# Value weights beside ones in an attention's second product, a guard term as a full-height product, and four-tap sums kept in PSUM

## The chip, the cores and the metric

The kernel runs on one core of one Trainium2 chip. The metric is the device time of one execution in microseconds (us), taken as the median of several runs. One execution was also recorded by the hardware profiler, and all rows below come from that recording. TensorE multiplies matrices, VectorE and ScalarE do elementwise work and can reach PSUM (the accumulators of TensorE), GpSimd does elementwise work in SBUF alone, and SyncE issues most of the transfers.

## What is computed

The reference is a two-layer backbone over 1024 latent tokens and 256 context tokens, all in float32, with a model width of 1024. Each layer has a token mixer of two parallel halves and then a gated feed-forward part. The change touches layer 1's mixer: its recurrence and its latent attention. It also touches how PSUM is handed out.

```python
def rglru_direction(u_lat, u_ctx, conv_w, conv_b, gate_w, gate_b, lam, reverse):
    pad = (0, LRU_CONV_WIDTH - 1) if reverse else (LRU_CONV_WIDTH - 1, 0)   # width 4
    def coeffs(u):
        xc = dwconv(u, conv_w, conv_b, pad[0], pad[1])                       # four taps
        r = jax.nn.sigmoid(block_diag(xc, gate_w[0], gate_b[0]))
        i = jax.nn.sigmoid(block_diag(xc, gate_w[1], gate_b[1]))
        ...
    h_lat = linear_scan(a_l, b_l, h0, reverse)

def one_block(args):                                   # 8 heads, 64 + 32 features
    s_lat = (einsum('bqhd,bshd->bhqs', qn, k_nope) + einsum('bqhr,bsr->bhqs', qr, k_rope)) * scale
    s_ctx = (einsum('bqhd,bshd->bhqs', qn, kc_nope) + einsum('bqhr,bsr->bhqs', qrr, kc_rope)) * scale
    p_lat, p_ctx = joint_softmax([s_lat, s_ctx])
    return einsum('bhqs,bshd->bqhd', p_lat, v) + einsum('bhqs,bshd->bqhd', p_ctx, vc)
```

## The kernel before

**Precision.** Most matrix products are made of three fp32r products of a high and a low part (lines 305 to 307, and the score products of the attention). P·V, the row sums and the recurrence's gates are plain float32, which the profile records as two records for one product.

**Order of the work.** The program text gives a priority order. A planner in the framework then orders the instructions of each engine by that priority and by estimated costs, and each engine runs its list strictly in that order. Generators (`spawn`, `pump`, `next(side)`) interleave background work with the matrix products.

**Recurrence (`lru`, `taps`, from line 975).** While the projections of layer 1's mixer run, it works on four groups of 128 channels. For a group, `taps` loads 1283 columns (1024 latent, 3 between, 256 context) into `xb` and makes, for each of two directions, one first product (line 997) and three multiply-and-add instructions (line 1001) on VectorE, all with their sum in SBUF. The next group's taps are made in the middle of a group. The gates are float32 products of 128x128 weights (line 1019), and GpSimd multiplies the input gate with the convolved input (line 1022). Layer 0's convolution (line 640) uses the same multiply-and-add instruction, with its sum in a three-bank PSUM tile `ca`.

**Attention (`mla`, `head`, from line 1352).** Eight heads, two groups of 512 queries, ten tiles of 128 keys (eight latent, two context): 160 steps. A step makes scores in `st` (three fp32r products of 128x512; a context tile has a fourth of one row, line 1376, that subtracts the query's guard). ScalarE takes the exponential into `p` (line 1378). P·V (line 1362) has the 64 value columns of the head as weights, and splits the 512 queries into halves: one half lands in partitions 0 to 63 of the bank `po`, the other in 64 to 127, so two matmuls use different column halves of TensorE's array. The row sums of P are built by elementwise addition, by the letters of `ACC`: six tiles on GpSimd (five additions), four on VectorE (three additions), and one closing addition (line 1395). Then two products with a matrix of ones (line 1398) put the row sums into `po`, VectorE takes the reciprocal (128x256, line 1400) and multiplies twice (64x256, line 1404). The guard of the next queries (`guard`, lines 1305 to 1331) runs in between: products into `sx` (lines 1312 and 1317, two banks), whose maxima VectorE takes (lines 1313 and 1319). `side` and `tail` interleave the next head's projections, its guard and the last head's end with the present head's scores.

**PSUM.** There are eight banks. `psum_pools` closes the pools before and opens new ones. In the attention they are sx, st, po and mm, two banks each; around it mm has four and `big` two of two banks each. Layer 0's projections use `ca` in the place of `big`.

Of the kernel before, what the change touches and what calls it, by code (L numbers as in the profile page):

```python
# [11 lines left out]
F32 = mybir.dt.float32  # L12
# [39 lines left out]
CY = 7.0  # L52
VS = (2, 2, 2, 2, 3, 3, 3, 3, 1, 1)
GK = 1
ACC = "GVGGVGGVGV"
PVD = 4
PB1 = 6
VW = 3
# [41 lines left out]
def tile_backbone(ctx: ExitStack, tc: tile.TileContext, a: dict, out: bass.AP):  # L100
# [25 lines left out]
        return f"{s}{uid[0]}"  # L126

    psum_pools(mm=4)
    cap = ExitStack()
    psum["ca"] = cap.enter_context(tc.tile_pool(name="cap", bufs=1, space=PSUM))  # L130
    ctx.callback(lambda: psx[0].close())

    def page(shape, dt=F32, s="pg"):
        return pgp.tile(shape, dt, tag="pg", name=nm(s))
# [463 lines left out]
    def mixer0(hs, nxt, xs0):  # L598
        w = a["ab_w_in"][0]
        pc = ph[0]  # L600
        rcos, rsin = pc.tile([128, 1024], F32, name="rcos", bufs=1), pc.tile([128, 1024], F32, name="rsin", bufs=1)
        protr = pc.tile([128, 3, 128], F32R, name="protr", bufs=1)
        with tc.tile_pool(name="m0a", bufs=1) as pa:
            prep = proj0(hs, w, pa, rcos, rsin, protr, xs0)
        cap.close()
        psum["big"] = psx[0].enter_context(tc.tile_pool(name="big0", bufs=2, space=PSUM))
        cat = Lazy()
        with tc.tile_pool(name="m0b", bufs=1) as pb:
            attn0(pb, *prep, cat)
        ws[0] = "o0"  # L610
        with tc.tile_pool(name="m0o", bufs=8 * len(YPO)) as po:
            for i, g in enumerate(GO0):
                if i < 2:
                    spawn(cat.load(GO0[i + 1]), "cat")
                ys, sq, last = outproj(a["ab_w_out"][0], cat, g, (lambda g: [po.tile([128, 512], F32, tag="y", name=nm("y")) for _ in range(8)]) if g in YPO else (lambda g: acts(g, 8, F32, "y")), lambda g: PO0[g], range(7, -1, -1) if g in OR0 else None)
                drain("cat")
                spawn(update(0, g, ys, sq, 2, last, True, (0, 3, 4) if g < 2 else None, nxt, PU0[g]))
            pumping[0] = True
            while not posted >= {(0, g) for g in YPO}:
                advance(flows["norm"])  # L620
            pumping[0] = False

    def proj0(hs, w, pa, rcos, rsin, protr, xs0):
        def conv(i, U):
            wc = lambda k: cols("acw", k * 4 + i)
            A = psum["ca"].tile([128, 1536], F32, tag="ca", name=nm("ca"))[:, 0:CW]
            B = None
            S.activation(A, U[:, 15:15 + CW], AF.Identity, scale=wc(15), bias=cols("acb", i))
            taps = [k for k in range(31) if k != 15]
            pt, dt = taps[:PTAPS], taps[PTAPS:]  # L630
            nch = 6
            for c in range(nch):
                for k in pt[c::nch]:
                    P = pa.tile([128, CW], F32, tag="cp", name=nm("cp"), bufs=2)
                    G.tensor_scalar(P, U[:, k:k + CW], wc(k), 1.0, ALU.mult, ALU.mult)
                    if B is not None:
                        G.tensor_add(P, P, B)
                    B = P
                for k in dt[c::nch]:
                    V.scalar_tensor_tensor(A, U[:, k:k + CW], wc(k), A, ALU.mult, ALU.add)  # L640
                yield CY
            O = pa.tile([128, CW], F32, tag="co", name=nm("co"), bufs=2)
            V.tensor_add(O, A, B)
            for g in range(3):
                nc.sync.dma_start(cd[g][:, i], O[:, COFF[g]:COFF[g] + TOK[g]])
# [334 lines left out]
    def lru(todo, x5, GW, sp, tiny, done):  # L980
# [4 lines left out]
        def taps(i):  # L985
# [7 lines left out]
            for d in range(2):  # L993
                x = x5("xc", 4)[:, 0:XW]
                XC.append(x)
                tap = lambda k: cols("lcw", (d * 4 + k) * 4 + i)
                V.tensor_scalar(x, XB[:, 3:3 + XW], tap(0 if d else 3), cols("lcb", d * 4 + i), ALU.mult, ALU.add)
                for k in range(4):
                    o = k + 3 if d else k
                    if o != 3:  # L1000
                        V.scalar_tensor_tensor(x, XB[:, o:o + XW], tap(k), x, ALU.mult, ALU.add)
            return XC

        XN = None
# [46 lines left out]
    def mixer1(hs, nxt):  # L1051
# [6 lines left out]
        G.memset(KR[64:128], 0.0)  # L1058
        G.memset(KR[96:97, 0:SEQ], -1.0)
        wv = []  # L1060
        with tc.tile_pool(name="m1a", bufs=1) as pa:
            proj1(hs, w, pa, tab, KR, wv)
        with tc.tile_pool(name="m1b", bufs=1) as pb:
# [131 lines left out]
    def mla(pc, tab, KR, wv):  # L1195
# [39 lines left out]
        scale = float(96 ** -0.5)  # L1235
        Q = {}

        VA = pc.tile([128, 10, 512], F32, name="va")

        def v_all(side):  # L1240
            wh, wl = wv
            for t in range(10):
# [4 lines left out]
                for k in range(2):  # L1247
# [2 lines left out]
                    T.matmul(ps, ch, rh, start=k == 0, stop=False)  # L1250
                    T.matmul(ps, ch, rl, start=False, stop=False)
                    T.matmul(ps, cl, rh, start=False, stop=k == 1)
                (S.copy if t % 2 else V.tensor_copy)(VA[:, t], ps)

        def split_s(raw, key, after=None):
            hi, lo = (pc.tile([128, raw.shape[1], 128], F32R, tag=key + x, name=nm(key), bufs=1) for x in "hl")
# [28 lines left out]
        def q_piece(h, g):  # L1285
# [11 lines left out]
            qh, ql, qc = (x[:, sl] for x in Q[h])  # L1297
            S.copy(qh, q)
            V.tensor_sub(qc, q, f32(qh))
            G.tensor_sub(ql[0:96], q[0:96], f32(qh[0:96]))  # L1300
            yield


# [48 lines left out]
        def head(h, g):  # L1352
            qh, ql, qc = (x[:, OFF[g]:OFF[g] + 512] for x in Q[h])
            kh, kl, kc = K[h % NK]
            po = psum["po"].tile([128, 512], F32, tag="po", name=nm("po"))
            accs, P = {}, []

            def pv(t):
                p = P[t]
                v = VA[:, t, h * 64:h * 64 + 64]  # L1360
                for b in range(2):
                    T.matmul(po[64 * b:64 * b + 64, 0:256], v, p[:, 256 * b:256 * b + 256], start=t == 0, stop=t == 9)  # L1362

            for t in range(10):
                st = psum["st"].tile([128, 512], F32, tag="st", name=nm("st"))
# [5 lines left out]
                else:  # L1371
# [1 line left out]
                    T.matmul(st, b_, qh, start=True, stop=False)  # L1373
                    T.matmul(st, a_, qh, start=False, stop=False)
                    T.matmul(st, a_, qc, start=False, stop=False)
                    T.matmul(st, kh[96:97, 0:128], ql[96:97], start=False, stop=True)
                p = pc.tile([128, 512], F32, tag="p", name=nm("p"), bufs=PB1)
                S.activation(p, st, AF.Exp, scale=scale)
                P.append(p)
                e = ACC[t]  # L1380
                if e not in accs:
                    accs[e] = p
                else:
                    n = pc.tile([128, 512], F32, tag="ac" + e, name=nm("ac"), bufs=2) if accs[e] in P else accs[e]
                    (G if e == "G" else V).tensor_add(n, accs[e], p)
                    accs[e] = n
                if t % 2 and t > PVD:
                    pv(t - PVD - 1)
                    pv(t - PVD)
# [1 line left out]
            for t in range(10 - PVD, 10, 2):  # L1391
                pv(t)
                pv(t + 1)
                yield
            V.tensor_add(accs["V"], accs["V"], accs["G"])
            yield
            for b in range(2):
                T.matmul(po[64 * b:64 * b + 64, 256:512], ones[:, 0:64], accs["V"][:, 256 * b:256 * b + 256], start=True, stop=True)
            rs = pc.tile([128, 256], F32, tag="rs", name=nm("rs"), bufs=2)
            V.reciprocal(rs, po[:, 256:512])  # L1400
            p0 = 64 * (h % 2)
            for b in range(2):
                o = OFF[g] + b * 256
                V.tensor_mul(att[h // 2][p0:p0 + 64, o:o + 256], po[64 * b:64 * b + 64, 0:256], rs[64 * b:64 * b + 64])
            if h % 2 and g:
                nc.sync.dma_start(attd[:, h // 2], att[h // 2])

        W, att, guarded, now = {}, {}, set(), [0]
        side = leads()
        psum_pools(sx=2, st=2, po=2, mm=2)  # L1410
        v_all(side)
        tail = iter(())
# [18 lines left out]
        for _ in tail:  # L1431
            pass
        drain("mul")
        psum_pools(big=2, mm=4)
        cat = Lazy()

        def load(g):
# [359 lines left out]
```

## Time and profile before

| | us |
|---|---|
| median of 3 runs | 3179.36 |
| lowest and highest | 3178.3, 3186.16 |
| profiled execution | 3171.12 |
| its span, first to last instruction | 3169.3 |

Busy time over the span: TensorE 2983.8 us (94%), VectorE 1879.2 (59%), GpSimd 1130.6 (36%), ScalarE 1115.0 (35%). The mean granted clock of TensorE was 0.966 of 2.4 GHz; it stands at either 1.2 or 2.4 GHz. A busy share counts a matmul from its start to its modelled end, and matmuls overlap, so the distance from start to start tells more of TensorE's stream than the busy time.

### The profile page before, as it was taken

How to read it: one execution, taken by the hardware profiler on the slowest of the kernel's cores; microseconds unless marked ns; L12 is line 12 of the kernel's file. 1: busy time of each engine (PE TensorE's matmuls, PEld its weight loads, DVE VectorE, ACT ScalarE, POOL GpSimd, SP SyncE). 2: the span in 40 equal slices, each digit the busy share in tenths (PEclk: the TensorE clock that was granted, in tenths of full speed). 3: DMA queues.
4: the chain of work that ended last, by engine and by line, in shares of the span. 5: the costliest groups of instructions: out<-in, count | busy, mean ns of one | idle time of the engine just before them, and what ended most of it. 6: DMA issues, size and time to landing. Idle time of an engine off the chain costs nothing. (4 is left out here: it accounts for less than half of the span.)

```text
span 3169.3 us, 38550 instructions
## 1 busy us (share of the span) xinstructions
PE 2983.8 (94%) x14825; PEld 2351.7 (74%) x14825; DVE 1879.2 (59%) x2842; ACT 1115.0 (35%) x1653; POOL 1130.6 (36%) x809
## 2 busy tenths in 40 slices
PE   6997999799999999988999779999998999999998
PEld 4886767678888888888987555555586888888886
DVE  5899986674654545577556977677636222223234
ACT  5214874532122111245533753233344322111213
POOL 4666546810111001165442344434444222122223
PEclk8998999899999999999999889999998999999999
DMA  7442004432333233346544230000053121111212
GB/s 283 130 135 91 28 15 143 144 109 73 94 100 93 75 90 102 113 147 202 159 132 130 89 98 26 31 31 27 33 167 100 53 60 47 33 48 54 60 40 106
DMA packets 321269, 292.50 MB, mean 92 GB/s; under 512 B 26065, under 2 KB 279678, under 8 KB 321086
## 3 DMA queue, kind: packets, MB, share of 16 engines
q1 hardware_dynamic: 317280, 287.14, 28.8%
q10 hardware_dynamic: 3806, 2.91, 0.3%
q8 instruction: 116, 1.90, 0.2%
q14 instruction: 67, 0.55, 0.1%
HBM read 243.82 MB, written 46.14 MB: 91 GB/s over the span
## 5 line engine op out<-in xcount | busy, mean ns | idle before, releaser
L288 POOL TENSOR_TENSOR wl<-wr,wh 128x1024 fp32r<-128x1024 f32 x165 | 405.8, 2460 | 1309.4 <-ACT wh L285 1285.0
L285 ACT CAST wh<-wr 128x1024 fp32r<-128x1024 f32 x270 | 281.9, 1048 | 1074.0 <-PE big L306 679.0
L305 PE MATMUL big<-hh,wh 128*128 128x512 f32 x1376 | 539.6, 393 | 3.1 <-ACT hh L487 1.6
L306 PE MATMUL big<-hl,wh 128*128 128x512 f32 x1376 | 537.0, 391 | 0.9 <-POOL hl L492 0.8
L307 PE MATMUL big<-hh,wl 128*128 128x512 f32 x1376 | 536.7, 390 | 0.6 <-DVE wl L288 0.6
L305 PE MATMUL mm<-hh,wh 128*128 128x256 f32 (+1 forms) x1000 | 347.7, 348 | 3.3 <-ACT hh L491 1.5
L307 PE MATMUL mm<-hh,wl 128*128 128x256 f32 (+1 forms) x1000 | 339.7, 340 | 5.8 <-DVE wl L288 3.7
L306 PE MATMUL mm<-hl,wh 128*128 128x256 f32 (+1 forms) x1000 | 340.6, 341 | 4.0 <-POOL hl L492 2.7
L305 PEld LDWEIGHTS big<-hh,wh 128*128 128x128 f32 x1376 | 259.3, 189 | 59.1 <-ACT hh L487 3.4
L306 PEld LDWEIGHTS big<-hl,wh 128*128 128x128 f32 x1376 | 259.4, 188 | 56.9 <-POOL hl L492 3.2
L307 PEld LDWEIGHTS big<-hh,wl 128*128 128x128 f32 x1376 | 259.2, 188 | 55.1 <-DVE wl L288 1.0
L1535 PE MATMUL mm<-zh,wh 128*128 128x512 f32 x704 | 276.7, 394 | 1.3 <-ACT xt L1626 0.7
L1536 PE MATMUL mm<-zl,wh 128*128 128x512 f32 x704 | 274.8, 390 | 0.3 <-DVE zl L312 0.3
L1537 PE MATMUL mm<-zh,wl 128*128 128x512 f32 x704 | 274.8, 390 | 0.0
L1542 DVE TENSOR_TENSOR acc<-acc,mm 128x512 f32<-128x512 f32 x224 | 150.8, 685 | 182.5 <-PE mm L1537 182.4
L462 POOL TENSOR_TENSOR sq<-t,sq 128x512 f32<-128x512 f32 (+1 forms) x153 | 198.3, 1299 | 161.4 <-ACT t L458 145.8
L1470 DVE SCALAR_TENSOR_TENSOR ga<-big,C,ga 128x1023 f32<-128x1023 f32 x86 | 110.2, 1281 | 234.1 <-ACT ga L1483 232.9
L288 DVE TENSOR_TENSOR wl<-wr,wh 128x1024 fp32r<-128x1024 f32 x105 | 157.0, 1497 | 106.3 <-ACT wh L285 97.2
L305 PEld LDWEIGHTS mm<-hh,wh 128*128 128x128 f32 x1000 | 194.0, 194 | 30.0 <-issue 4.2
L306 PEld LDWEIGHTS mm<-hl,wh 128*128 128x128 f32 x1000 | 193.5, 194 | 28.6 <-POOL hl L492 5.5
L307 PEld LDWEIGHTS mm<-hh,wl 128*128 128x128 f32 x1000 | 193.3, 193 | 27.0 <-DVE wl L288 4.3
L388 DVE SCALAR_TENSOR_TENSOR wa<-wm,sc,wa 128x256 f32<-128x256 f32 x280 | 152.5, 572 | 89.9 <-DMA wm<-in_w_mod_dram 87.4
(354 smaller groups left out, 5497.0 us busy)
## 6 DMA issues: line engine op xcount, KB each, us to landing
wr<-in_ffn_w_up_dram SPq DMA_DIRECT2D x132, 512.0 KB, 3.9
wr<-in_ffn_w_down_dram SPq DMA_DIRECT2D x66, 512.0 KB, 3.7
wm<-in_w_mod_dram SPq DMA_DIRECT2D x224, 128.0 KB, 2.1
wm<-in_w_mod_dram SPq DMA_DIRECT2D x40, 512.0 KB, 7.4
xd<-x SPq DMA_DIRECT2D x38, 512.0 KB, 5.2
x<-xd SPq DMA_DIRECT2D x38, 512.0 KB, 7.1
wr<-in_ab_w_out_dram SPq DMA_DIRECT2D x24, 512.0 KB, 7.1
wr<-in_cd_w_in_dram SPq DMA_DIRECT2D x17, 512.0 KB, 3.9
```

The source lines that it names most:

```text
L285: S.copy(hi[:, 0:nk, 0:m], raw[:, 0:nk, 0:m])
L288: (G if e[wn[0] % len(e)] == "G" else V).tensor_sub(lo[:, 0:nk, 0:m], raw[:, 0:nk, 0:m], f32(hi[:, 0:nk, 0:m]))
L305: T.matmul(ps, wh, xh[k], start=i == 0, stop=False)
L306: T.matmul(ps, wh, xl[k], start=False, stop=False)
L307: T.matmul(ps, wl, xh[k], start=False, stop=i == n - 1)
L388: V.scalar_tensor_tensor(acc[:, v], raw, sc[:, k, v:v + 1], acc[:, v], ALU.mult, ALU.add)
L462: self.eng.tensor_add(self.acc[-1], t, self.acc[-1])
L1470: V.scalar_tensor_tensor(dst[:, lo:hi], src[:, lo + d - o:hi + d - o], k, dst[:, lo:hi], ALU.mult, ALU.add)
L1535: T.matmul(ps, wh, zh, start=j == j0, stop=False)
L1536: T.matmul(ps, wh, zl, start=False, stop=False)
L1537: T.matmul(ps, wl, zh, start=False, stop=j == j1 - 1)
L1542: V.tensor_add(ys[g][c], ys[g][c], ps)
```

## The change

P·V gets weights of 128 columns: a head's 64 values beside 64 columns of ones (even heads: values, ones; odd heads: ones, values), so that one product of 128x512 gives the weighted values in one half of `po`'s partitions and the row sums in the other half, in the place of two of 64 columns. The elementwise row sums and the products with ones go. The reciprocal is taken over 64x512 and one multiplication of 64x512 follows. The value tile has room for the ones, which GpSimd writes. The guard term of a context tile is a product of all 128 rows, with a weight tile E that is -1 in row 96 and 0 elsewhere; GpSimd writes E, and the low part of the query, `ql`, is written in all 128 partitions. The recurrence's taps keep their running sum in a three-bank PSUM tile, the last one writing to SBUF; the tile stands where `big` stood, for the time of the projections. After the attention, mm is opened ahead of `big`.

```diff
-ACC = "GVGGVGGVGV"
     psum_pools(mm=4)
-    cap = ExitStack()
-    psum["ca"] = cap.enter_context(tc.tile_pool(name="cap", bufs=1, space=PSUM))
+    psy = [ExitStack()]
+    def psum_side(key, n):
+        psy[0].close()
+        psy[0] = ExitStack()
+        psum[key] = psy[0].enter_context(tc.tile_pool(name=nm(key), bufs=n, space=PSUM))
+    def wide():
+        return psum["ca"].tile([128, 1536], F32, tag="ca", name=nm("ca"))
+    psum_side("ca", 1)
...
-                V.tensor_scalar(x, XB[:, 3:3 + XW], tap(0 if d else 3), cols("lcb", d * 4 + i), ALU.mult, ALU.add)
-                for k in range(4):
+                A = wide()[:, 0:XW]
+                V.tensor_scalar(A, XB[:, 3:3 + XW], tap(0 if d else 3), cols("lcb", d * 4 + i), ALU.mult, ALU.add)
+                ks = (1, 2, 3) if d else (0, 1, 2)
+                for k in ks:
                     o = k + 3 if d else k
-                    if o != 3:
-                        V.scalar_tensor_tensor(x, XB[:, o:o + XW], tap(k), x, ALU.mult, ALU.add)
+                    V.scalar_tensor_tensor(x if k == ks[-1] else A, XB[:, o:o + XW], tap(k), A, ALU.mult, ALU.add)
...
         wv = []
+        psum_side("ca", 1)
...
-        VA = pc.tile([128, 10, 512], F32, name="va")
+        VA = pc.tile([128, 10, 4, 3, 64], F32, name="va")
+        for t in range(10):
+            G.memset(VA[:, t, :, 1], 1.0)
+        E = pc.tile([128, 128], F32R, name="gd")
+        G.memset(f32(E), 0.0)
+        G.memset(f32(E[96:97]), -1.0)
...
-                (S.copy if t % 2 else V.tensor_copy)(VA[:, t], ps)
+                (S.copy if t % 2 else V.tensor_copy)(VA[:, t, :, ::2], ps.rearrange("p (a b m) -> p a b m", b=2, m=64))
...
-            G.tensor_sub(ql[0:96], q[0:96], f32(qh[0:96]))
+            G.tensor_sub(ql, q, f32(qh))
...
             def pv(t):
-                p = P[t]
-                v = VA[:, t, h * 64:h * 64 + 64]
-                for b in range(2):
-                    T.matmul(po[64 * b:64 * b + 64, 0:256], v, p[:, 256 * b:256 * b + 256], start=t == 0, stop=t == 9)
+                v = VA[:, t, h // 2, h % 2:h % 2 + 2].rearrange("p b m -> p (b m)")
+                T.matmul(po, v, P[t], start=t == 0, stop=t == 9)
...
-                    T.matmul(st, kh[96:97, 0:128], ql[96:97], start=False, stop=True)
+                    T.matmul(st, E, ql, start=False, stop=True)
...
-                e = ACC[t]
-                if e not in accs:
-                    accs[e] = p
-                else:
-                    n = pc.tile([128, 512], F32, tag="ac" + e, name=nm("ac"), bufs=2) if accs[e] in P else accs[e]
-                    (G if e == "G" else V).tensor_add(n, accs[e], p)
-                    accs[e] = n
...
-            V.tensor_add(accs["V"], accs["V"], accs["G"])
+            rs = pc.tile([128, 512], F32, tag="rs", name=nm("rs"), bufs=2)
+            p0 = 64 * (h % 2)
+            V.reciprocal(rs[p0:p0 + 64], po[64 - p0:128 - p0])
             yield
-            for b in range(2):
-                T.matmul(po[64 * b:64 * b + 64, 256:512], ones[:, 0:64], accs["V"][:, 256 * b:256 * b + 256], start=True, stop=True)
-            rs = pc.tile([128, 256], F32, tag="rs", name=nm("rs"), bufs=2)
-            V.reciprocal(rs, po[:, 256:512])
-            p0 = 64 * (h % 2)
-            for b in range(2):
-                o = OFF[g] + b * 256
-                V.tensor_mul(att[h // 2][p0:p0 + 64, o:o + 256], po[64 * b:64 * b + 64, 0:256], rs[64 * b:64 * b + 64])
+            V.tensor_mul(att[h // 2][p0:p0 + 64, OFF[g]:OFF[g] + 512], po[p0:p0 + 64], rs[p0:p0 + 64])
...
+        psy[0].close()
         psum_pools(sx=2, st=2, po=2, mm=2)
...
-        psum_pools(big=2, mm=4)
+        psum_pools(mm=4)
+        psum_side("big", 2)
```

## Rows read from the trace of the kernel before

**Rows 1.** Stretches: length, each engine's busy us (instructions), granted clock, DMA share, GB/s.
```profile
1755.00:1830.00 75.00, 61.95 (x215) 42.52 (x216) 73.85 (x72) 53.61 (x61) 29.97 (x15) 0.91 0.28 89
...
1916.00:2297.00 381.00, 367.40 (x1568) 200.24 (x1567) 274.05 (x367) 126.10 (x219) 159.33 (x148) 0.96 0.09 30
```

**Rows 2.** Timeline of TensorE from 2122.66: start, duration, instruction, count.
```profile
2122.66 0.39 PE L1370 MATMUL st<-q,kh 97*128 97x512 f32 x1
2122.98 1.08 PE L1362 MATMUL po<-p,va 128*64 128x256 f32 x8
2123.99 0.50 PE L1373 MATMUL st<-q,kc 128*128 128x512 f32 x1
2124.33 0.39 PE L1374 MATMUL st<-q,kc 128*128 128x512 f32 x1
2124.56 0.40 PE L1375 MATMUL st<-q,kc 128*128 128x512 f32 x1
2124.89 0.50 PE L1376 MATMUL st<-q,kh 1*128 1x512 f32 x1
2125.32 0.50 PE L1373 MATMUL st<-q,kc 128*128 128x512 f32 x1
```

**Rows 3.** Timeline of TensorE from 2056.04, a block of two.
```profile
2056.04 0.65 PE L1362 MATMUL po<-p,va 128*64 128x256 f32 x2
2056.62 0.50 PE L1368 MATMUL st<-q,kl 96*128 96x512 f32 x1
```

**Rows 4.** Line 1362: count, duration min/median/max in ns, first and last start.
```profile
L1362 PE MATMUL po<-p,va x640: 379/379/689, 1916.9 to 2292.9; 128*64 128x256 f32 x160
```

**Rows 5.** Timeline of TensorE, the recurrence's gates: one block, another's end.
```profile
1714.92 3.17 PE L1019 MATMUL mm<-xc,gw 128*128 128x512 f32 x8
...
1724.32 1.02 PE L1019 MATMUL mm<-xc,gw 128*128 128x512 f32 x3
...
1725.42 0.28 PE L307 MATMUL mm<-hh,wl 128*128 128x256 f32 x1
```

**Rows 6.** Groups in the attention, 1916 to 2297: busy us, mean ns, idle before.
```profile
L1385 DVE TENSOR_TENSOR ac<-ac,p 128x512 f32<-128x512 f32 x32 | 31.1, 971 | 11.3 <-ACT p L1378 10.8
...
L1400 DVE RECIPROCAL rs<-po 128x256 f32<-128x256 f32 x16 | 28.1, 1754 | 13.0 <-PE po L1398 12.9
...
L1385 POOL TENSOR_TENSOR ac<-ac,p 128x512 f32<-128x512 f32 x64 | 86.7, 1355 | 64.2 <-ACT p L1378 62.8
```

**Rows 7.** Timelines of VectorE and TensorE around 2004; idle before and its releaser.
```profile
2003.47 1.74 DVE L1395 TENSOR_TENSOR ac<-ac,ac 128x512 f32<-128x512 f32 x1 [3.20 <-POOL ac L1385]
...
2006.47 0.50 PE L1317 MATMUL sx<-kc,q 128*128 128x256 f32 x2 [2.56 <-DVE mt L1313]
```

**Rows 8.** Stretch behind that wait, as in the first group.
```profile
2007.70:2021.40 13.70, 13.70 (x34) 7.62 (x34) 6.32 (x10) 2.58 (x5) 2.94 (x3) 0.50 0.05 19
```

**Rows 9.** Groups of VectorE from 1700 to 1815: the taps.
```profile
L1001 DVE SCALAR_TENSOR_TENSOR xc<-xb,C,xc 128x1283 f32<-128x1283 f32 x24 | 49.5, 2100 | 0.3
L997 DVE TENSOR_SCALAR xc<-xb,C 128x1283 f32<-128x1283 f32 x8 | 12.5, 1583 | 5.6 <-DMA xb<-xbd 5.6
```

**Rows 10.** Lines 997 and 640 (layer 0's convolution): count, min/median/max ns.
```profile
L997 DVE TENSOR_SCALAR xc<-xb,C x8: 935/949/3554, 1701.1 to 1805.4; 128x1283 f32<-128x1283 f32 x8
...
L640 DVE SCALAR_TENSOR_TENSOR ca<-u,C,ca x88: 1555/1571/1573, 98.6 to 294.7; 128x1295 f32<-128x1295 f32 x88
```

**Rows 11.** Timelines of VectorE and GpSimd from 1759: taps beside a GpSimd product.
```profile
1759.40 5.67 DVE L1001 SCALAR_TENSOR_TENSOR xc<-xb,C,xc 128x1283 f32<-128x1283 f32 x2
...
1760.27 3.45 POOL L1022 TENSOR_TENSOR i<-i,xc 128x1283 f32<-128x1283 f32 x1 [2.85 <-issue]
```

**Rows 12.** Timelines of GpSimd and TensorE at the attention's start and end.
```profile
1872.86 0.74 POOL L1258 TENSOR_TENSOR wk<-wr,wk 128x256 fp32r<-128x256 f32 x1 [3.62 <-issue]
...
2296.54 0.47 PE L305 MATMUL mm<-ch,wh 128*128 128x512 f32 x1 [2.85 <-DVE att L1404]
```

**Rows 13.** Line 1155, a GpSimd memset: count, min/median/max ns.
```profile
L1155 POOL MEMSET stg<- x1: 524/524/524, 1825.0 to 1825.0; 128x512 f32 x1
```

More of the change, by code (lines that the diff above doesn't have):

```diff
@@ L128, in tile_backbone @@
     psum_pools(mm=4)
-    cap = ExitStack()
-    psum["ca"] = cap.enter_context(tc.tile_pool(name="cap", bufs=1, space=PSUM))
+    psy = [ExitStack()]
[6 more added lines that the diff above has]
+    psum_side("ca", 1)
     ctx.callback(lambda: psx[0].close())
+    ctx.callback(lambda: psy[0].close())
     def page(shape, dt=F32, s="pg"):
@@ L604, in mixer0 @@
             prep = proj0(hs, w, pa, rcos, rsin, protr, xs0)
-        cap.close()
-        psum["big"] = psx[0].enter_context(tc.tile_pool(name="big0", bufs=2, space=PSUM))
+        psum_side("big", 2)
         cat = Lazy()
@@ L625, in conv @@
             wc = lambda k: cols("acw", k * 4 + i)
-            A = psum["ca"].tile([128, 1536], F32, tag="ca", name=nm("ca"))[:, 0:CW]
+            A = wide()[:, 0:CW]
             B = None
@@ L1355, in head @@
             po = psum["po"].tile([128, 512], F32, tag="po", name=nm("po"))
-            accs, P = {}, []
+            P = []
             def pv(t):
-                p = P[t]
-                v = VA[:, t, h * 64:h * 64 + 64]
-                for b in range(2):
-                    T.matmul(po[64 * b:64 * b + 64, 0:256], v, p[:, 256 * b:256 * b + 256], start=t == 0, stop=t == 9)
+                v = VA[:, t, h // 2, h % 2:h % 2 + 2].rearrange("p b m -> p (b m)")
+                T.matmul(po, v, P[t], start=t == 0, stop=t == 9)
             for t in range(10):
@@ L1433, in mla @@
         drain("mul")
-        psum_pools(big=2, mm=4)
+        psum_pools(mm=4)
+        psum_side("big", 2)
         cat = Lazy()
```

## The prediction, made before the changed kernel was run

> **What bounds the kernel now.** The page's busy shares come first: TensorE has the highest by far, so an edit pays only where it shortens TensorE's own stream or a stretch in which TensorE waits. The table by stretch then places the two halves of the change [rows 1]. From 1916 to 2297 us (layer 1's attention) TensorE is busy for 367.4 of 381 us, VectorE for 274, GpSimd for 159. There TensorE's stream is the bound, and the reader should look at what lies between the starts of its matmuls, since a busy share hides that. From 1755 to 1830 us (the recurrence) VectorE is busy for 73.85 of 75 us and TensorE for 62. There VectorE's queue is the bound.
>
> **How I read the stream.** At full clock an fp32r matmul of 512 columns starts 0.23 us after the one before it (2124.33 to 2124.56 in [rows 2]). Blocks of P·V matmuls, with 64 columns of weights, break that rhythm. In the block of eight [rows 2] the matmul before it is followed after 0.32 us instead of 0.23, the block lasts 1.01 us, and the matmul behind it takes 0.34 instead of 0.23: 1.01 + 0.09 + 0.11 = 1.21 us for two key tiles. A block of two, one half of one tile, is worse [rows 3]: 2056.04 to 2056.62 is 0.58, plus the same 0.09 before and 0.10 behind, 0.77 us, and its partner half pays it again. The planner often put guard matmuls (sx) between the halves.
>
> Going through the timeline from the first P·V matmul at 1916.9 to the last at 2292.9 us (640 records, [rows 4]) I find 61 blocks of two (0.77 us each), 31 of eight (1.21), 27 of six (1.21; it lasts as long as eight), 19 of four (0.88), and 21 blocks that hold the 64 row-sum matmuls, some with P·V among them (24.2 us in all). Sum: 47.2 + 37.4 + 32.5 + 16.8 + 24.2 = 158 us at full clock.
>
> **P·V with ones beside the values.** After, each of the 160 (head, group, key tile) has one product with 128 columns of weights over 512 columns of P, and no row-sum matmuls. The same form stands in the recurrence's gates, plain float32, 128x128 weights: two records for each product. In [rows 5] eight of them, six of 512 columns and two of 256, take 3.17 us with the last one's 0.17 us of running out: 0.428 us from start to start at 512 columns, 0.214 at 256. Leaving such a block costs nothing: from 1724.32 one record of 512, two of 256 and two fp32r matmuls of 256 (0.12 each) should take 0.428 + 0.428 + 0.24 = 1.10 us, and the next starts at 1725.42, 1.10 later. So 320 × 0.428 = 137 us against 158: -21 us, all of it on TensorE's path. Bounds: -13 if the half-clock and waiting parts of my blocks are counted too high, -28 if the half-clock stretches, where both prices double, are charged in full.
>
> The Trainium skill has a rule against this half (TensorEngine Tiling (Array Packing), Theoretical Speedup): weights of at most 64 columns can run as two tiles at up to twice the rate. By it, as an estimate, the old form would need about 69 us and the change would add about 68. The trace agrees only inside a block, where eight records take the time of four. Its Key Properties say that a change of tiling mode drains the engine, and the 0.09 and 0.10 us around each block agree with that.
>
> **The guard term.** The one-row matmul of a context tile starts 0.33 us after its predecessor and holds the next back by 0.43 [rows 2]; the one after that again takes 0.34. With E in full height all would be 0.23. 19 of the 32 are followed by another score matmul (0.33 + 0.43 + 0.34 - 0.70 = 0.40 each), 13 by a P·V block whose entry I counted already (0.19): -10 us. A 128-row fp32r matmul of this shape is in the same rows, so the price is certain within 1 us.
>
> **VectorE and GpSimd in the attention.** Gone are 48 VectorE sums and 16 closing sums at about 0.97 us (62 us) and 80 GpSimd sums at 1.35 (106 us) [rows 6]. Two 64x256 multiplications become one of 64x512, no dearer. The reciprocal goes from 256 to 512 columns on half the partitions. 256 columns cost 1.754 us [rows 6]; doubled that is 3.5, and if partitions counted it would stay 1.75. The other rows of this engine go by columns, so I take 3.4: +26 us. VectorE falls from 274 to some 238 us and GpSimd to 53, both off TensorE's path, so I credit nothing for them. Together with the waits they could still give something: at 2003.4 us GpSimd reached a sum late, VectorE's closing sum waited for it, and TensorE stood for 2.56 us behind the guard's maxima [rows 7]; then came 13.7 us at half clock, 1.2 GHz [rows 8]. The stage's granted clock of 0.96 [rows 1] means some 28 us at half, which cost 14; 381 less 14, and less the 350 us that all its matmuls take at the full-clock spacings above, leaves 17 us of waits. Value 0; bounds -25 and, if the long reciprocals bring more waits, +14.
>
> **The four-tap sums.** VectorE's 24 SBUF sums take 49.5 us, 2.10 each, and the eight first products 12.5 [rows 9]. The means hide two kinds: most sums take 1.55 us, and five about 4.2, each while a GpSimd product of 128x1283 ran. The pair of sums at 1759.40 took 5.67 us, and GpSimd worked from 1760.27 to 1763.72 [rows 11]. Layer 0's convolution does the same instruction with its sum in PSUM, 88 times, beside GpSimd work: 1555 to 1573 ns, never longer [rows 10]. So 24 × 1.57. The first product with PSUM as its destination is not in the trace: between 0.94 (undisturbed, SBUF) and 1.57 (the sum) [rows 10], I take 1.5, the dearer row being nearer in operands. 62.0 - 37.7 - 12.0 = -12.3 us of busy time, and neighbours overlap a little, so some 10 of VectorE's queue. Of these the share of the first of three disturbed groups is partly lost, because VectorE waited there for ScalarE. On the path: -8 us, bounds 0 (GpSimd then collides with the next two-input instruction) and -14. The three banks come from the pool "big", which nothing uses in this phase; the projections keep their four.
>
> **Small things.** GpSimd gets ten memsets of 128x256 and two for E: the one like them takes 0.524 us for 512 columns [rows 13], so 10 × 0.27 + 0.2 = 3 us, queued ahead of the key-weight split, for which TensorE and VectorE wait at the stage's start; GpSimd idles 3.6 us just before it [rows 12], which covers them if their memory is free by then; if not they cost up to 3. +1 us. The value copies keep their 512 elements: 0. The wider ql difference has the same columns: 0. At the stage's end TensorE waits 2.85 us for the final multiplication, since the output projection's first bank was the last head's [rows 12]. With the pools in the new order its banks are those of the scores, free earlier, but the longer reciprocal delays the last piece of the input by 1.6 - 0.6 us: -2, bounds -3 and +1.
>
> **Sum.** -21 - 10 + 0 - 8 + 1 - 2 = -40 us. The profiled execution took 3171.1 us (span 3169.3 and 1.8 around it), 8.2 us under the median of the runs, 3179.4. I carry the difference over to the median: 3139 us.
>
> **Rivals.** (a) The waits and half-clock stretches go too: GpSimd's sums caused the one I followed. Another -25: 3114. For it: two thirds of GpSimd's work leaves. Against: other stretches began without it. (b) What surrounds a P·V block is not the tiling but the change between plain float32 and fp32r, and stays: some 140 blocks × 0.19 = +27, so 3166. The gates' block, left without an extra, speaks against it [rows 5]. (c) Slower: the 3.4 us reciprocal sits in VectorE's queue between guard maxima, TensorE's next guard matmul has two banks and then waits, and each such wait brings a half-clock stretch like the one in [rows 8]. Price: 1.6 + 6.9 us for each of 16 (head, group) pairs, 136 in all, so 3179 - 40 + 136 = 3275; it decides from five pairs on. Against: the old closing sum, row sums and reciprocal already took about as long in a row. (d) The taps don't escape GpSimd: 3147, within my own range.
>
> **How the numbers follow.** Forecast with (d) 0.69; (a) 0.14; (b), or a gain eaten by a few new waits, 0.10, half of it within 0.3%; (c) 0.07. Range: 3108 for (a) with the full tap gain, to 3166 for (b). 0.3% (9.5 us) is about what a measurement of this kernel can tell from no change. Faster 0.88, same 0.05, slower 0.07.
>
> **What would show it.** In the attention stretch of after: P·V records 0.428 us apart with 0.23 around them, the stage 31 us shorter, VectorE near 238 us busy, reciprocals of 3.4 us. In the recurrence: no tap above 1.6 us and the stretch 8 us shorter. I am wrong if reciprocals stand ahead of TensorE's waits, if the granted clock in the stage falls below its 0.96, or if float32 records are wider apart than in the gates.

## The result and the profile after

| | us |
|---|---|
| kernel before, median beside the first runs of after | 3178.83 |
| changed kernel, median of 4 runs (lowest, highest) | 3127.55 (3120.31, 3135.68) |
| ratio, with 95% interval | 0.9844 [0.9821, 0.9868], about -50 us |
| the same, measured a second time | 3131.08, ratio 0.9861 [0.9842, 0.988], about -44 us |
| profiled executions of after (span 3133.9, and 3131.4 the second time) | 3135.68, 3133.24 |

So the change gains 44 to 50 us; 40 was forecast. The profiled execution of before lies 8 us under its median and that of after 8 us above, so the two differ by 35 us only. I therefore go by stages, and by more than one profile of each kernel.

The stretches of after that answer to [rows 1] are those below: length, busy us (instructions) of TensorE, its weight loads, VectorE, ScalarE and GpSimd, granted clock, DMA share, GB/s. In the recurrence VectorE has 62 of 75 us, where it had 73.85. In the attention TensorE is still the bound, VectorE fell from 274 to 216 us, GpSimd from 159 to 52, and the granted clock rose from 0.96 to 0.99.

```profile
1749.00:1824.00 75.00, 64.32 (x241) 45.65 (x242) 62.14 (x73) 56.79 (x67) 27.54 (x15) 0.91 0.29 93
1913.00:2259.00 346.00, 337.56 (x1180) 212.89 (x1179) 216.09 (x284) 125.71 (x218) 51.69 (x69) 0.99 0.10 33
```

TensorE's timeline of after around a P·V block of two key tiles answers to [rows 2, 3]. From the block's start to the next matmul are 1.32 us, and from there to the one after 0.64: 1.96 in all, which is 4 × 0.428 + 0.24. This block of plain float32 products with 128 columns of weights has neither entry nor exit.

```profile
2126.05 0.40 PE L1386 MATMUL st<-q,kh 97*128 97x512 f32 x1
2126.28 1.88 PE L1378 MATMUL po<-p,va 128*128 128x512 f32 x4
2127.60 0.80 PE L1384 MATMUL st<-q,kl 96*128 96x512 f32 x1
2128.24 0.40 PE L1385 MATMUL st<-q,kh 96*128 96x512 f32 x1
```

The single lines of after: count, duration min/median/max in ns, first and last start. They answer to [rows 4, 6, 9, 10, 13].

```profile
L1378 PE MATMUL po<-p,va x320: 590/592/1055, 1913.1 to 2258.4; 128*128 128x512 f32 x160
...
L1392 PE MATMUL st<-q,gd x32: 387/394/628, 1921.9 to 2253.4; 128*128 128x512 f32 x32
...
L1406 DVE RECIPROCAL rs<-po x16: 3342/3355/3360, 1931.9 to 2259.0; 64x512 f32<-64x512 f32 x16
...
L1007 DVE TENSOR_SCALAR ca<-xb,C x8: 1606/1614/1619, 1702.7 to 1794.5; 128x1283 f32<-128x1283 f32 x8
...
L1011 DVE SCALAR_TENSOR_TENSOR ca<-xb,C,ca x16: 1547/1558/1560, 1704.6 to 1797.7; 128x1283 f32<-128x1283 f32 x16
L1011 DVE SCALAR_TENSOR_TENSOR xc<-xb,C,ca x8: 1539/1550/1552, 1709.0 to 1799.3; 128x1283 f32<-128x1283 f32 x8
...
L1252 POOL MEMSET va<- x10: 311/311/311, 1859.2 to 1861.5; 128x256 f32 x10
```

The guard's product is now a matmul like its neighbours (394 ns). The reciprocal takes 3.36 us. No tap takes more than 1.62 us, where five of the sums had taken about 4.2.

What TensorE waited for in the attention of after (from the first to the last P·V product: us in total, times, longest). The first line is one wait, the largest of the stage.

```profile
PE sx L1330 <- DVE mt L1331: 4.0, 1, 4.0
PE sx L1330 <- ACT q L1316: 2.5, 6, 0.8
PE st L1386 <- issue: 0.7, 1, 0.7
PE st L1386 <- DMA q<-m: 0.6, 1, 0.6
```

In before the guard's context tiles waited for VectorE's maxima seven times in that stretch:

```profile
PE sx L1317 <- DVE mt L1313: 7.2, 7, 2.6
```

### The profile page after: what moved, and what is told of

It is laid out like the page before. It is cut to its first block, busy times and chain, and to the rows that moved or that the text cites. A ratio compares the mean times of both kernels' runs of the same rounds, so it can differ in the third digit from the quotient of the medians.

```text
span 3133.9 us, 37547 instructions
## 1 busy us (share of the span) xinstructions
PE 2951.0 (94%) x14441; PEld 2361.4 (75%) x14441; DVE 1819.8 (58%) x2762; ACT 1114.5 (36%) x1653; POOL 1020.1 (33%) x741
```

## The experiments

The table has one profile of each kernel in its first three columns of numbers: from the first P·V product's start to the last one's end, how much of that TensorE had 1.2 GHz by the trace's record of the clock, and the length less half of that, which is the length at full clock. The ratio is that of the runs to those of the kernel before beside them.

| kernel | P·V first to last, us | at 1.2 GHz | at full clock | median | ratio |
|---|---|---|---|---|---|
| before | 376.3 | 27.3 | 362.7 | 3178.83 | 1 |
| before, again | 394.4 | 61.4 | 363.6 | 3189.39 (one run) | |
| taps alone | 373.5 | 17.1 | 365.0 | 3162.17 | 0.9966 [0.9951, 0.998] |
| P·V with ones alone | 358.7 | 10.2 | 353.6 | 3155.19 | 0.9935 [0.9921, 0.9949] |
| guard alone | 356.2 | 6.8 | 352.8 | 3156.49 | 0.9933 [0.9917, 0.9948] |
| changed, guard undone | 359.2 | 13.7 | 352.4 | 3143.76 | 0.9902 [0.9884, 0.9919] |
| changed | 345.8 | 6.8 | 342.4 | 3127.55 | 0.9844 [0.9821, 0.9868] |
| changed, again | 344.7 | 3.4 | 343.0 | 3131.08 | 0.9861 [0.9842, 0.988] |
| changed, pool order undone | 345.7 | 6.8 | 342.3 | 3133.78 | 0.9869 [0.9844, 0.9895] |
| changed, GpSimd's sums kept | 354.1 | 6.8 | 350.7 | 3136.92 | 0.9877 [0.9848, 0.9905] |
| changed, short reciprocal | 343.2 | 3.4 | 341.5 | 3122.7 | 0.9837 [0.9813, 0.9861] |
| halves side by side | 349.0 | 30.7 | 333.6 | 3124.12 | 0.9843 [0.9823, 0.9863] |
| the same, blocks later | 347.9 | 27.3 | 334.3 | 3124.87 | 0.9844 [0.9822, 0.9865] |
| changed, six products on GpSimd | 339.9 | 0 | 339.9 | 3124.27 | 0.9821 [0.9797, 0.9846] |

**The taps alone.** The kernel before with the recurrence's edit and nothing else:

```diff
-                V.tensor_scalar(x, XB[:, 3:3 + XW], tap(0 if d else 3), cols("lcb", d * 4 + i), ALU.mult, ALU.add)
+                A = wide()[:, 0:XW]
+                V.tensor_scalar(A, XB[:, 3:3 + XW], tap(0 if d else 3), cols("lcb", d * 4 + i), ALU.mult, ALU.add)
...
+                    V.scalar_tensor_tensor(x if k == ks[-1] else A, XB[:, o:o + XW], tap(k), A, ALU.mult, ALU.add)
```

> The kernel before with one edit: the recurrence's four-tap sums of layer 1 stand in PSUM; P.V, row sums, guard term and pool order of the projections are as before. My theory (GpSimd's products stretched five sums, and PSUM escapes that): the recurrence's last scan ends 6 to 8 us earlier, no tap above 1.62 us, the whole 8 us shorter (3171 beside 3179). Rival (the eight microseconds are caught up at the attention's start by something else that is late): last scan earlier but the first P.V matmul as late as before, 0 us.

The ratio is 11 us (6 to 16). From the first tap to the last scan it took 148.1 us; the four profiles that have the old taps show 159.0, 161.1, 159.1 and 159.1, the ten with the new ones 148.1 to 150.9. The attention's first P·V then starts 16.5 us earlier than in the profile of before, and 5.1 of that stood already ahead of the first tap, so the gain is not caught up. My theory holds, with a last scan 10 us nearer to the first tap and not 6 to 8.

**P·V with ones alone.**

```diff
-                for b in range(2):
-                    T.matmul(po[64 * b:64 * b + 64, 0:256], v, p[:, 256 * b:256 * b + 256], start=t == 0, stop=t == 9)
+                T.matmul(po, v, P[t], start=t == 0, stop=t == 9)
```

> The kernel before with one edit: value weights beside ones, 128 columns, one product for each (head, group, key tile), no row sums added on VectorE and GpSimd; taps in SBUF, one-row guard term. My theory: the attention's matmul stream is 21 us shorter, and the whole 21 to 28 us (3151 to 3158). Rival (a), freed VectorE and GpSimd and the half-clock stretches go too: 35 to 45 us (3134 to 3144). Rival (c), waits behind the long reciprocal: less than 10 us.

21 us (16 to 25), as my theory had it, but not where it had it. At full clock the stage is 10 us shorter than in before (353.6 and 362.7 to 365.0), and the rest is less time at 1.2 GHz: 10.2 us against 17 to 61. The runs without a profile agree: each one's span times one less its mean granted clock, which is the time that the lower clock cost it, is 99 us in the mean of these 5 and 108 in the 17 of before beside them.

**The guard alone, and the change without it.**

```diff
-                    T.matmul(st, kh[96:97, 0:128], ql[96:97], start=False, stop=True)
+                    T.matmul(st, E, ql, start=False, stop=True)
```

> The kernel before with one edit: the guard's one-row matmul takes weights of 128 rows (E, one row of it not zero). My theory: 10 us shorter (3169), from 19 places of 0.40 us and 13 of 0.19 us. Rival (the one-row matmul's extra time hides behind the P.V blocks' own entry and exit, and only part shows): 0 to 4 us.

> The changed kernel with the one-row guard matmul back. With no P.V blocks of 64 columns beside it every one of the 32 should cost 0.40 us. Theory A (the guard term is worth its matmul time and nothing more): 11 to 15 us slower than the changed kernel, and the full-clock length of the attention stage grows by 13. Theory B (the one-row matmuls also bring half-clock stretches of their own, which is where the guard alone found 21 and not 10 us): 18 to 25 us slower, with some 20 us more of half clock in the attention.

At full clock the guard is worth 11 us alone (352.8 against a mean of 363.8 for the three profiles with everything old in the attention) and 10 beside the new P·V (352.4 with the old guard, 342.4 and 343.0 with the new). That is the 10 us of the forecast. In the whole time it was 21 us alone (17 to 26) and 13 to 18 beside the new P·V. The difference is again time at 1.2 GHz: the kernels with one of the two edits have 6.8 to 13.7 us of it, those with both 3.4 to 6.8. Theory B wanted 20 us of half clock for the one-row products; there are 7 to 10, so theory A is the nearer, although it had put 13 us at full clock where 10 came.

**The kernel before once more.**

> The kernel before once more, one profile, to see how far the half-clock stretches of the attention vary between executions of one kernel. If they belong to the order of work: again 20 to 30 us at half clock between the first and the last P.V matmul. If they come and go: under 14.

61 us, above both ranges. Its waits are those of the first profile at the same places, with one more of 2.5 us at 2277, behind a sum on VectorE that took 4.60 us where the others take 0.7 to 1.8: TensorE stood 2.56 us until 2006.6 (2.56 until 2006.5 in the first), 0.78 until 2152.4 (0.62 until 2150.6), 1.71 until 2213.7 (1.70 until 2204.3). What follows them differs. The stretches of this second profile:

```profile
2007.40:2024.40 17.00, 17.00 (x42) 9.23 (x43) 8.17 (x12) 3.01 (x6) 3.81 (x3) 0.50 0.04 15
2154.10:2171.20 17.10, 17.10 (x43) 7.75 (x42) 7.17 (x14) 1.76 (x3) 1.11 (x1) 0.50 0.00 1
2215.60:2232.60 17.00, 17.00 (x42) 8.13 (x41) 7.52 (x11) 2.39 (x4) 2.54 (x2) 0.50 0.00 1
```

and two of the first, which answer to the second and third of them (the first one's answer is [rows 8], 13.7 us at 0.50):

```profile
2152.40:2169.40 17.00, 17.00 (x80) 9.93 (x79) 13.02 (x22) 6.93 (x12) 3.52 (x3) 1.00 0.12 32
2205.70:2209.10 3.40, 3.40 (x11) 1.51 (x9) 1.89 (x3) 0.60 (x1) 0.00 (x0) 0.50 0.00 0
```

Much the same short wait is followed by 1.2 GHz for 17 us in one execution and not at all in the other. So the stage of the kernel before varies by 18 us between two executions with hardly a change of its length at full clock (362.7 and 363.6). An edit that takes such waits away also takes away what sometimes follows them, and that part of the gain can't be read from one profile.

**GpSimd's sums kept.** The changed kernel still issues GpSimd's 80 additions of P, and nothing reads them; the output is complete without them.

```diff
+                if e == "G":
...
+                        G.tensor_add(n, accs[e], p)
```

> The changed kernel, with GpSimd's 80 additions of P (the old row sums' part) still issued; nothing reads their results. It tells what the freed GpSimd is worth. My theory (0 credited): within 5 us of the changed kernel. Rival (a) (GpSimd's sums slowed VectorE's guard maxima and reciprocals and so caused waits and half-clock stretches): 10 to 25 us slower than the changed kernel, half clock in the attention back to over 20 us from 7.

The stage is 8 us longer at full clock, the whole 5 to 11 us slower by the ratios, whose intervals overlap. By the stage neither expectation was right: it is more than nothing, and none of it is half clock (6.8 us, as without the sums). The maxima (687 ns) and the reciprocals (3354 ns) kept their length too. It is waits, mostly for the next head's query:

```profile
PE sx L1331 <- ACT q L1317: 9.5, 9, 2.3
PE sx L1331 <- DVE mt L1332: 3.3, 2, 2.6
```

In the changed kernel the first of these is 2.5 us. TensorE waits there for ScalarE's rounding of the query, and that waits for VectorE, which rotates 32 rows of the query with instructions whose inputs are both in SBUF. The waits of ScalarE and the first of those instructions, in the changed kernel and then in this one:

```profile
ACT q L1316 <- DVE t L1313: 12.5, 14, 1.6
L1311 DVE TENSOR_TENSOR t<-t,tab 32x512 f32<-32x512 f32 x14 | 11.7, 836 | 40.0 <-ACT t L1310 39.9
```

```profile
ACT q L1317 <- DVE t L1314: 19.2, 14, 2.9
L1312 DVE TENSOR_TENSOR t<-t,tab 32x512 f32<-32x512 f32 x14 | 14.4, 1025 | 39.5 <-ACT t L1311 39.5
```

ScalarE's wait grew by 6.7 us, TensorE's by 7.0. VectorE's subtraction behind the rounding, 128x512 with two inputs in SBUF, shows the same. These are its groups in the attention of before, of the changed kernel, and of this one (busy us, mean ns):

```profile
L1299 DVE TENSOR_TENSOR q<-t,q 128x512 fp32r<-128x512 f32 x14 | 18.4, 1317 | 4.5 <-ACT q L1298 4.4
```

```profile
L1317 DVE TENSOR_TENSOR q<-t,q 128x512 fp32r<-128x512 f32 x14 | 9.7, 692 | 8.2 <-ACT q L1316 8.1
```

```profile
L1318 DVE TENSOR_TENSOR q<-t,q 128x512 fp32r<-128x512 f32 x14 | 12.3, 879 | 8.2 <-ACT q L1317 8.1
```

Beside GpSimd's sums it takes 1.3 or 0.9 us, without them 0.69. The Trainium skill (SBUF — State Buffer, Who interferes with whom) says that a VectorE instruction with two inputs in SBUF contends with a GpSimd instruction that reads SBUF. These rows agree, and so do the taps, whose second input is now in PSUM.

The experiment leaves one path out: nothing here reads the sums, so VectorE has no closing sum that could wait for them, as it did in [rows 7].

**A short reciprocal.** The reciprocal is taken of 256 of the 512 columns and used for both halves, so half of the columns are divided by another column's sum.

```diff
-            V.reciprocal(rs[p0:p0 + 64], po[64 - p0:128 - p0])
+            V.reciprocal(rs[p0:p0 + 64, 0:256], po[64 - p0:128 - p0, 0:256])
```

> The changed kernel, with the reciprocal taken of 256 of the 512 columns and used for both halves (so half the columns are divided by another column's row sum): 16 reciprocals of 1.75 us and not 3.35. TensorE stands 32 us in all behind values that follow a reciprocal or for their banks by the profile's account, of which most is no real wait. My theory: 0 to 7 us faster than the changed kernel. Rival (c) in a small form (the long reciprocal is what the remaining 21 us of waits come from): 12 to 20 us faster.

16 × 1.6 us leave VectorE's queue and the stage gets 1 us shorter at full clock, the whole 2 to 8 us by the ratios. The long reciprocal is not what TensorE waits for; rival (c) falls.

**The pool order undone.**

```diff
-        psum_pools(mm=4)
-        psum_side("big", 2)
+        psum_pools(big=2, mm=4)
```

> The changed kernel with the old order of the PSUM pools in layer 1's output projection (its first banks are those of the last head's P.V). My theory: TensorE waits about 2.8 us for the last multiplication before the output projection, as it did before the change, and a longer one behind the 3.4 us reciprocal: 1 to 4 us slower than the changed kernel. Rival: the banks make no difference, since the projection's input is the last piece anyway: within 1 us of it.

With the old order the output projection begins 4.26 us after the last P·V, at the last multiplication. In the changed kernel it follows at once. The two kernels' rows:

```profile
2261.08 0.77 PE L315 MATMUL mm<-ch,wh 128*128 128x512 f32 x1 [4.26 <-DVE att L1408]
```

```profile
2258.39 0.79 PE L315 MATMUL mm<-ch,wh 128*128 128x512 f32 x1
```

But from the last P·V to the end of the projection's last matmul it is 100.9 us at full clock with the old order, and 100.9 and 99.0 in the two profiles with the new: in the first of them the wait comes back inside, behind weights and the last piece of the input, in five stops of 3.1 us together. (In the two profiles of before the same length is 98.5 and 97.8.) The 3 to 8 us of the ratios lie mostly in stages that the edit doesn't touch (in this profile layer 0 has 123 us at 1.2 GHz, in those of the changed kernel 96 and 113). Theory and rival can't be told apart at this size; the stage's own lengths are nearer to the rival.

**The halves side by side.** If short blocks made the old P·V dear, the old form in long blocks should beat the ones. This is the changed kernel with 64 columns of weights and elementwise row sums again, and the eight records of two key tiles issued together:

```diff
+            def pair(t0):
+                with shifted(-4000):
+                    for t in (t0 + 1, t0):
...
+                        for b in range(2):
+                            T.matmul(po[64 * b:64 * b + 64, 0:256], v, p[:, 256 * b:256 * b + 256], start=t == 1, stop=t == 8)
```

> The changed kernel with the old form of P.V put back (64 columns of weights, two column halves, row sums added on VectorE and GpSimd) but with the matmuls of two key tiles always issued side by side, eight records in a block, so that a block's entry and exit are paid 80 times and not in 61 blocks of two. My theory (what made the old form dear was the splitting into short blocks): 80 blocks of two key tiles at 1.21 us and 16 row-sum blocks at 0.9 us are 111 us of stream against 137 in the changed kernel, so 26 us less stream; with the row sums back on VectorE and GpSimd up to 17 us of waits come with it: 9 to 26 us faster than the changed kernel (3102 to 3119). Rival (the change was right to leave the halves, since they cost more than the records show, or since the sums make TensorE wait): no faster than the changed kernel, 3128 or more.

The stream did what was expected. Its blocks of eight, with a median of 1.014 us (76 of 80 came out whole):

```profile
2151.39 0.40 PE L1388 MATMUL st<-q,kh 97*128 97x512 f32 x1
2151.72 1.08 PE L1380 MATMUL po<-p,va 128*64 128x256 f32 x8
2152.74 0.50 PE L1386 MATMUL st<-q,kl 96*128 96x512 f32 x1
2153.08 0.40 PE L1387 MATMUL st<-q,kh 96*128 96x512 f32 x1
```

Counted from start to start, without the listed waits, all P·V and row-sum blocks with their entries and exits take 110 us, against 142 for P·V by the same count in the changed kernel. The stage is only 9 us shorter at full clock, and 24 us more of it at 1.2 GHz take that back, so the whole is level with the changed kernel. TensorE now reaches what it needs before it is there:

```profile
PE po L1380 <- ACT p L1396: 4.8, 9, 2.1
PE st L1386 <- ACT p L1396: 4.3, 8, 1.0
PE sx L1328 <- ACT q L1314: 3.0, 3, 1.4
PE st L1388 <- DMA q<-m: 3.0, 5, 1.2
```

Its waits are 22 us in all, those of the changed kernel 8. The Trainium skill's rule that weights of at most 64 columns can run at up to twice the rate (TensorEngine Tiling (Array Packing), Theoretical Speedup) is borne out in direction, 110 for 142 with the entries counted. On this kernel it buys no time.

> The kernel with the two halves side by side in blocks of eight records, with the blocks two key tiles later behind their scores (and eight buffers for P in place of six). My theory (pulling the blocks together put them too close behind the exponentials, and TensorE waits for these): 3 to 10 us faster than with the lag of four tiles (3114 to 3121). Rival (the waits come from the next head's preparation and from VectorE's sums, not from the lag): within 3 us of it, 3121 to 3127, or slower.

The edit there is `PVD = 6` for 4 and `PB1 = 8` for 6. Nothing moved, at full clock or in the waits (22 us of idle TensorE in both). A longer lag did not help.

**The last large wait.** The 4 us wait of the changed kernel stands behind a multiplication of the recurrence's output in VectorE's queue, whose input was still on its way:

```profile
1946.26 0.69 DVE L1135 TENSOR_TENSOR t<-t,t 128x512 f32<-128x512 f32 x1 [4.34 <-DMA t<-hsd]
...
1947.61 0.80 PE L1330 MATMUL sx<-kh,q 96*128 96x512 f32 x1 [3.99 <-DVE mt L1331]
```

```diff
-                    V.tensor_mul(t, t, t2)
+                    (G if late else V).tensor_mul(t, t, t2)
```

`late` holds for the second group of channels on: six of the eight multiplications.

> The changed kernel, with six multiplications of the recurrence's output (128x512, both inputs by DMA) moved from VectorE's queue to that of GpSimd, which the change has left two thirds empty. In both profiles of the changed kernel one of them stands 4 us at the head of VectorE's queue waiting for its DMA (1946 us), the guard's maxima stand behind it, TensorE waits 3.8 to 4.0 us for them, and the attention's only half-clock stretch follows. Theory (a wait is worth its own length and the half-clock stretch behind it): attention 4 to 7 us shorter (338 to 341 us from first to last P.V matmul, half clock 0 to 3.4 us), the whole 4 to 8 us faster than the changed kernel (3120 to 3126). Rival (TensorE then waits for the next query, whose subtraction now stands behind a DMA in GpSimd's queue): no gain, waits behind ACT's or GpSimd's q grow by 4 us or more.

The stage came out at 339.9 us with a granted clock of 1.00. Its row, and what TensorE still waits for:

```profile
1910.30:2250.20 339.90, 335.05 (x1179) 210.51 (x1178) 213.07 (x278) 125.77 (x218) 59.30 (x75) 1.00 0.11 33
```

```profile
PE sx L1330 <- ACT q L1316: 2.9, 7, 0.8
PE st L1386 <- issue: 0.6, 1, 0.6
PE st L1386 <- DMA q<-m: 0.6, 1, 0.6
PE sx L1335 <- DVE mt L1331: 0.2, 1, 0.2
```

The wait for the query grew by 0.4 us and not by 4, so the rival falls. At 0.9821 it is the fastest kernel of the study; its interval overlaps that of the changed kernel, so that it beats it is shown in the stage (5 us in one profile against two, 3 of them at full clock) and only likely in the whole.

## Why the prediction was right, and where it was not

The direction and the size were right (-40 forecast, -44 and -50 measured, both inside the range). The sum has two wrong terms of opposite sign, 10 us too much and 15 too little, so that the total came out so near is in part luck. The sign that I had named, a stage 31 us shorter, was met in length (376.3 to 345.8 us), but only 20 us of that are at full clock.

**P·V with ones: -21, measured -10 to -11 at full clock.** The step that failed is the sum of 158 us over the old blocks. The trace of before gives, with the block prices of the forecast, 121 us inside the blocks (61 of two at 0.576, 31 of eight at 1.014, 27 of six at 1.008, 19 of four at 0.583, 16.5 for those with row sums). Entries were paid 146 times at 0.094 and exits 153 times at 0.104, not at all 159 blocks, and some of them at 1.2 GHz, where they count half: 29 us. That makes 150. I had charged an entry to blocks behind a one-row product, which pay none, an exit to blocks ahead of a transpose, which pay none, 0.1 us too much to each block of four, and waits for the row sums to the row-sum blocks. The bound of -13 that I gave for just this was the better value. A block of eight, at 1.01 us, also takes the time of nearly five records at 0.214 us and not of four.

The new half was right where nothing else interferes: 0.428 us apart, no entry and no exit. But over the whole stage the 320 records take 142 us from start to start without the listed waits, not 137: behind some blocks the next matmul starts up to 0.6 us late, and the profile lists no wait there, since the last record of P·V covers most of it. So the stream got 8 us shorter, and the listed waits fell from 11 us in before to 8, which makes the 11. With GpSimd's sums kept the changed kernel had 7 us more of listed waits, so the freed GpSimd has its part in that fall; how large a part, the runs don't settle.

**Guard term: -10, measured -10 and -11 at full clock.** Right.

**VectorE and GpSimd freed, waits and half clock: 0, measured about -15.** This is the other failed step, and it is half of rival (a). The three profiles with the old attention have 27.3, 61.4 and 17.1 us at 1.2 GHz, a mean of 35; the two of the changed kernel have 6.8 and 3.4. Half of the difference is 15 us. Profiles of one kernel lie far apart in this, but the runs bear it out: the cost of the lower clock (span times one less the granted clock) is 109 us in the mean of 11 runs of before and 92 in the 4 of the changed kernel beside them, and of these 18 us the profiles put about 4 in the recurrence.

I had read the 28 us of one profile as a cost, but credited the change with none of it, because some stretches began without a wait for GpSimd's sums. In the three profiles with the old attention every stretch begins during a wait of TensorE for the guard's maxima, or up to 2 us behind one, and what VectorE did before those maxima was work that the change removes or shortens. The longest wait stood behind a closing sum that waited for GpSimd [rows 7]. It is still there with the guard alone, where the sums are still made:

```profile
2001.53 1.73 DVE L1409 TENSOR_TENSOR ac<-ac,ac 128x512 f32<-128x512 f32 x1 [3.21 <-POOL ac L1399]
...
2004.53 0.80 PE L1331 MATMUL sx<-kc,q 128*128 128x256 f32 x2 [3.15 <-DVE mt L1327]
```

It is gone in every kernel without a closing sum. Another in before stood behind the subtraction of 128x512, which took 2.98 us beside a subtraction and an addition on GpSimd:

```profile
2200.55 2.98 DVE L1299 TENSOR_TENSOR q<-t,q 128x512 fp32r<-128x512 f32 x1
...
2204.31 0.51 PE L1317 MATMUL sx<-kc,q 128*128 128x256 f32 x2 [1.70 <-DVE mt L1313]
```

So rival (a) had the cause of these waits right, and the experiment with GpSimd's sums kept, which has no closing sum, doesn't speak against it. The waits for the maxima are 7.2 us in seven in before, 3.6 in two with the guard alone, and 4.2 in one with P·V alone. Why the guard's edit removes the smaller ones the runs don't show; the planner orders every kernel anew. That the stretches come from the waits is read from where they begin; the last experiment, in which the wait went and no stretch was left, agrees in one profile.

**Taps: -8, measured -10.** The first product into PSUM took 1.61 us (1.5 forecast), the sums 1.55 (1.57), and GpSimd held none of them up. Rival (d) falls.

**Memsets: +1, pool order: -2, measured 0 and about +2.** Ten memsets of 0.311 us (0.27 forecast) stood behind a DMA and ended at 1861.8, and from the last scan to the first P·V it is 48.4 us at full clock in the mean, as before (48.2). The stage's end did not gain: from the last P·V to the end of the output projection it is 100 us at full clock in the mean, where it was 98. The wait ahead of the projection went, but others came behind it.

Sum of what was measured: -11 - 10 - 15 - 10 + 0 + 2 = -44 us, the smaller of the two gains of the changed kernel; the 15 is known to some 5 us only. The three parts alone add up to 53, each with 5 us of uncertainty; half clock that either of two parts removes would be in both.

**Rivals.** (b) falls by the timeline around a P·V block. (c) had its duration right (3.4 forecast, 3.36 measured), but TensorE doesn't wait behind the reciprocal: half its length taken away gave 1 us. VectorE fell to 216 us and not to 238, mostly since its instructions with two inputs in SBUF got faster (the subtraction from 18.4 to 9.7 us).

## What to carry to other kernels

Price a stream by the distances from start to start and count entries and exits one by one: a sum over hundreds of blocks with a tenth of a microsecond too much at each is out by as much as a whole edit. Before crediting nothing to freed engines, list the waits of the bound engine and the half-clock stretches behind them, in more than one profile: what follows a wait can be longer than the wait, and an edit that removes the wait gets both. When a bound engine's stream gets shorter still, look first for an instruction at the head of another queue that waits for a DMA; moving it to an idle engine made the stage 5 us shorter here, for one line.

## What was not expected of the hardware

- The same wait of TensorE at the same place was followed by 13.7 us at 1.2 GHz in one execution and 17.0 in another, and one of 0.6 to 0.8 us by none and by 17.1.
- VectorE's 128x512 subtraction with both inputs in SBUF took 1.32 us on average beside GpSimd's 80 additions, 0.69 without them.
- A float32 product by a scalar of 128x1283 into PSUM took 1.61 us, as much as a sum of two inputs (1.55), while into SBUF it took 0.95 undisturbed [rows 10].
